# Where the scheduler may reorder a hybrid layer: projection by a timeline model, attention and the down projection in the order they are written

## The chip, the cores and the metric

The kernel runs on one core of a Trainium2 chip. The metric is the device time of one execution in microseconds, as the median of several runs. A core has TensorE (PE, matrix products into the PSUM banks), VectorE (DVE), ScalarE (ACT), GpSimd (POOL) and SyncE (SP, which here issues the DMAs). Each engine works through its own list of instructions in the order of that list, and semaphores hold an instruction until its inputs are there. What the change alters is these lists.

## The reference, cut to what matters

One layer of a decoder trunk, over one sequence of 2048 positions with 1024 channels in float32:

```python
mod = silu(c) @ W_ada + b_ada        # shift, scale and gate, twice
h = RMSNorm(x) * (1 + scale1) + shift1
p = h @ W_in                          # one projection for all head groups
#  A  mLSTM, 4 heads x 64, chunks of 64
#  B  forgetting attention, 8 heads x 64
#  C  spatial gating, 4 groups x 64, chunks of 128
x = x + gate1 * (concat(A, B, C) @ W_out)
h = RMSNorm(x) * (1 + scale2) + shift2
x = x + gate2 * ConvFFN(h)            # up (1024 -> 5632), conv of width 3, SwiGLU, down (2816 -> 1024)

def forgetting_attention(q, k, v, f_pre):     # for each block of 128 queries
    F = cumsum(log_sigmoid(f_pre))
    logits = einsum('bhtd,bhsd->bhts', qb, kb) * scale + F[..., lo:hi, None] - F[..., None, :hi]
    p = softmax(where(mask, logits, -inf))
    out = einsum('bhts,bhsd->bhtd', p, vb)
```

## The kernel before, in words

All products are made in a split form: every operand is cut into a high part hi (fp32r) and a rest lo, and `mm3` (L53 to L56) issues three matmuls, hi·hi, hi·lo and lo·hi. Matmuls named acc belong to the projection, wps to the out-projection, ub to up, db to Down. PSUM tiles are small in number, and each pool of tiles has a fixed count of buffers; an instruction that writes a buffer waits until the last reader of its former content is done.

**Projection** (0 to about 745 us of the trace). Rows of x are normed (ACT squares them, L569, DVE scales them, L571), transposed on PE into tiles trp (L605), and cut into hi and lo. Blocks of weights of w_in come by DMA into wr, ACT makes wh (L652, L676), DVE or POOL makes wl (L653, L677), and PE accumulates. The results are normed (qn L846, vhl L830) and written to DRAM. mLSTM and spatial gating run as lanes between these products. The loop over the steps (L1191 on) is entered, from its second step on, under `tc.manual_schedule` for PE, DVE, ACT and POOL: there these engines' lists follow the program's text. Everything else is put in order by the scheduler of the tile framework, which runs a list schedule against a model of the machine.

**Attention** (about 745 to 1183 us). Heads are taken one after the other; a head is four blocks of 512 query rows, tb = 0 to 3, and block tb attends to (tb + 1) · 512 keys. `scores` makes, for each of four rows of 128 queries, one or two score tiles sp of up to 1024 keys: matmuls (L206, and L210 for the causal mask), a reduction on DVE that adds the forget bias, writes the tile L and tracks the row's minimum nm (L212), and then `exps`: one exp per tile on ACT with its sum rs (L223), the sum's inverse on POOL (L225, L226) and a scaling of the tile on POOL (L228). For tb = 2 and 3 a row has two tiles, so there are eight steps a block, and a row's exps need the reductions of both tiles. `finish` takes the rows of a block and makes, for each 128 keys j, four transposes into a tile tp (L259), a cast phi on ACT (L262), a difference plo on DVE (L263), and, three steps later, two products into op (L245, L246). At the end of a block ACT copies op to yo (L250). PSUM holds two score tiles, three tp and one op. `phase` interleaves the score steps of one block with the finish steps of the block before. Splits of the weights w_out (wo0, L131 and L132) are written between phases of the last heads.

**Out-projection** to 1390 us, **up** to about 2250 us (seven products p of a Strassen-like scheme for each of 22 groups and two halves of the rows, prepared on DVE and ACT: wsph L1467, wspl L1468).

**Down** (about 2241 us to the end). Two halves H of the rows; in each the products p = 1, 2, 7, 6, 5, 4, 3, each of 11 steps k. A step is twelve matmuls of 512 columns into four banks. `prep` makes its operands: sums on DVE (L1577 to L1593, according to p), then for both operands hi on ACT (wsph, L1598) and lo on DVE (wspl, L1599). `prep` is called three steps ahead of `mm`, and the twelve buffers of wsp hold three steps. `post` puts the evictions of a product in the list `later` (copies s1 L1652, sums o, u2 and s1 in L1633 to L1689), and of this list three items are taken after each step. The banks are db0 and db1 in turn; p = 3 goes on accumulating in the tile of p = 5.

## Time and profile before

| | |
|---|---|
| median of 3 runs | 2671.54 us (2666.39 to 2672.4) |
| the profiled execution, time | 2675.71 us |
| the profiled execution, span | 2674.0 us |
| mean granted clock of TensorE | 0.988 |
| POOL busy | 415.6 us, 550 instructions |
| HBM read, written | 274.34 MB, 100.74 MB |

The page of the profile gives for each engine the busy time and its share of the span. A view of stretches gives the same for pieces of the span, with the clock that TensorE was granted there. The view of waits lists, for each place where an engine stood idle, what ended the wait. The timeline lists instructions in order of time: start, duration, engine, line, operation, output and inputs, and in brackets the idle time before it with what ended it. Starts of successive instructions of one engine lie closer than their durations, since they overlap; where a rate matters, the distance of starts is used.

### The profile page before, as it was taken

Reading aid. Unit: us, or ns where it says so; the run is one execution under the profiler, and the core shown is the slowest. Engines: PE = TensorE matmul, PEld = TensorE weight load, DVE = VectorE, ACT = ScalarE, POOL = GpSimd, SP = SyncE. Lnnn points to the kernel's source line nnn. Section 1 sums busy time; section 2 is a strip of 40 time slices with the busy share of each in tenths; the row PEclk is TensorE's granted clock in tenths of the full one; section 3 lists DMA queues with packets and bytes.
Section 4 is the critical chain, followed back from the end, with each engine's and each line's share of the span. In section 5 each row is a group of like instructions: output and inputs, shape, how many; then the busy total and the mean of one; then the engine's idle time right before and its main releaser. Section 6 shows DMA issues by size and latency. Waiting matters only on the chain.

```text
span 2674.0 us, 36818 instructions
## 1 busy us (share of the span) xinstructions
PE 2580.6 (97%) x12761; PEld 2128.9 (80%) x12761; DVE 1992.1 (75%) x3432; ACT 1285.4 (48%) x2442; POOL 415.6 (16%) x550
## 2 busy tenths in 40 slices
PE   5899999999899999999999999999999999999999
PEld 5788787888777877777877888888888888888787
DVE  5555656455448888876749888887988887898797
ACT  3333334333248788874436544444444444444443
POOL 4012210022236566640000000000000000000000
PEclk9899999999999999999999999999999999999999
DMA  7533556424554444536742222228222225748533
GB/s 257 154 117 91 150 152 184 132 70 123 138 171 123 115 133 125 136 98 229 276 142 72 90 84 84 82 84 294 89 85 82 84 79 206 267 148 308 177 101 116
DMA packets 297683, 377.52 MB, mean 141 GB/s; under 512 B 31118, under 2 KB 189676, under 8 KB 295448
## 3 DMA queue, kind: packets, MB, share of 16 engines
q1 hardware_dynamic: 297496, 375.16, 44.4%
q8 instruction: 101, 1.65, 0.3%
q14 instruction: 86, 0.70, 0.1%
HBM read 274.34 MB, written 100.74 MB: 140 GB/s over the span
## 4 chain that ended last, share of the span: by engine, by line
PE 74%; DVE 11%; DMA 5%; ACT 4%; issue 4%; POOL 1%; SPq 0%; DVEq 0%; ACTq 0%; POOLq 0%
PE ub L54 10%; PE ub L56 10%; PE ub L55 10%; PE acc L54 5%; PE acc L56 5%; PE acc L55 5%; PE db L55 4%; PE db L56 4%; PE db L54 4%; PE tp L259 3%; PE sp L206 3%; PE op L245 2%; PE op L246 2%; DVE wspl L1599 2%; DMA x_d<-x 1%
## 5 line engine op out<-in xcount | busy, mean ns | idle before, releaser
L54 PE MATMUL acc<-wh,hh 128*128 128x512 f32 (+2 forms) x768 | 290.8, 379 | 10.9 <-DVE vhl L830 5.3
L55 PE MATMUL acc<-wl,hh 128*128 128x512 f32 (+2 forms) x768 | 277.5, 361 | 4.5 <-POOL wl L677 3.4
L54 PE MATMUL ub<-T,wsph 128*128 128x512 f32 x704 | 274.3, 390 | 5.8 <-ACT wsph L1467 5.8
L56 PE MATMUL acc<-wh,hl 128*128 128x512 f32 (+2 forms) x768 | 278.1, 362 | 0.4 <-DVE hl L611 0.4
L56 PE MATMUL ub<-T,wspl 128*128 128x512 f32 x704 | 273.8, 389 | 0.4 <-DVE wspl L1468 0.4
L55 PE MATMUL ub<-T,wsph 128*128 128x512 f32 x704 | 273.9, 389 | 0.0
L55 PE MATMUL db<-wspl,wsph 128*128 128x512 f32 x616 | 240.4, 390 | 2.2 <-DVE wspl L1599 2.2
L56 PE MATMUL db<-wsph,wspl 128*128 128x512 f32 x616 | 239.6, 389 | 0.0
L54 PE MATMUL db<-wsph 128*128 128x512 f32 x616 | 238.3, 389 | 0.3 <-ACT wsph L1598 0.3
L1467 ACT CAST wsph<-S 128x512 fp32r<-128x512 f32 x176 | 109.7, 623 | 228.6 <-PE ub L55 162.5
L263 DVE TENSOR_TENSOR plo<-tp,phi 128x512 fp32r<-128x512 f32 (+1 forms) x320 | 186.8, 607 | 35.9 <-ACT phi L262 34.0
L54 PE MATMUL ub<-B,wsph 128*128 128x512 f32 x528 | 207.3, 393 | 2.6 <-ACT wsph L1467 2.6
L56 PE MATMUL ub<-B,wspl 128*128 128x512 f32 x528 | 207.0, 392 | 0.8 <-DVE wspl L1468 0.8
L55 PE MATMUL ub<-B,wsph 128*128 128x512 f32 x528 | 207.1, 392 | 0.0
L223 ACT ACTIVATE L<-L,nm 128x1024 f32<-128x1024 f32 (+2 forms) x192 | 172.5, 902 | 32.1 <-DVE nm L212 30.8
L259 PE MATMUL tp<-ident,L 128*128 128x128 f32 x1088 | 178.6, 276 | 5.2 <-DVE vhl L830 1.9
L262 ACT CAST phi<-tp 128x512 fp32r<-128x512 f32 (+1 forms) x320 | 160.1, 521 | 46.0 <-PE tp L259 44.7
L54 PEld LDWEIGHTS acc<-wh,hh 128*128 128x128 f32 x768 | 148.3, 193 | 32.3 <-issue 6.6
L206 PE MATMUL sp<-kk,q 128*128 128x512 f32 (+3 forms) x640 | 168.4, 374 | 2.3 <-DVE nm L212 1.2
L228 POOL TENSOR_SCALAR L<-L,rs 128x1024 f32<-128x1024 f32 (+2 forms) x192 | 167.2, 881 | 11.2
L1598 ACT CAST wsph<-act 128x512 fp32r<-128x512 f32 x132 | 82.2, 623 | 179.0 <-PE db L55 162.6
L55 PEld LDWEIGHTS acc<-wl,hh 128*128 128x128 f32 x768 | 148.2, 193 | 25.1 <-POOL wl L677 3.7
(344 smaller groups left out, 6025.8 us busy)
## 6 DMA issues: line engine op xcount, KB each, us to landing
w<-in_w_up_dram SPq DMA_DIRECT2D x88, 512.0 KB
wd<-in_w_down_dram SPq DMA_DIRECT2D x176, 256.0 KB
wa<-in_w_ada_dram SPq DMA_DIRECT2D x96, 256.0 KB
act_d<-yc SPq DMA_DIRECT2D x44, 512.0 KB
act<-act_d SPq DMA_DIRECT2D x44, 512.0 KB
wr<-in_w_in_dram SPq DMA_DIRECT2D x76, 256.0 KB
q<-q_d SPq DMA_DIRECT2D x128, 128.0 KB
hc_d<-hl SPq DMA_DIRECT2D x28, 512.0 KB
```

The lines of the kernel that those rows point to most:

```text
L54: T.matmul(ps, lh, rh, start=start, stop=False, skip_group_check=resume)
L55: T.matmul(ps, lh, rl, start=False, stop=False, skip_group_check=resume)
L56: T.matmul(ps, ll, rh, start=False, stop=stop, skip_group_check=resume)
L206: T.matmul(sp[:, b : b + bw], q2[n][:, qs], kk[:, s0 + b : s0 + b + bw], start=n == 0, stop=n == 1 and not last)
L223: A.activation(L[c], L[c], AF.Exp, bias=nm[:, n - 1 : n], scale=-1.0, accum_out=rs[:, c : c + 1])
L228: G.tensor_scalar(t, t, rs[:, 0:1], 1.0, op0=ALU.mult, op1=ALU.mult)
L245: T.matmul(op[:, c0:], vv[:, j, :], hi[:, c0:], start=(j == 0), stop=False)
L259: T.transpose(tp[:, i * P : (i + 1) * P], rows[i][j // 8][:, (j % 8) * P : (j % 8 + 1) * P], ident)
L262: A.copy(hi[:, c0:], tp[:, c0:])
L263: V.tensor_tensor(lo[:, c0:], tp[:, c0:], hi[:, c0:].bitcast(F32), op=ALU.subtract)
L1467: A.copy(hi, src)
L1598: A.copy(hi, v)
```

## The change

The scheduler's model is changed for the whole program (`schedule_with_timeline_sim=True`): it now orders against a timeline simulation. The manual schedule of the projection is removed, so that the projection's four engines are ordered by that model too. All PE, DVE, ACT and POOL instructions of attention, and the DVE and ACT instructions of Down, are wrapped in `tc.keep_in_program_order`, called O: each is put behind the one last wrapped on its engine, so that these follow the text among themselves, while other instructions may still go between. In Down the bank counter is also advanced for p = 3, so that the second half begins in the bank that the first half's last product does not hold. No instruction of computation is added or removed; out-projection and up stay free.

```diff
@@ mm3
+    O = tc.keep_in_program_order
@@ scores
-                        T.matmul(
+                        O(T.matmul(
                             sp[:, b : b + bw], q2[n][:, qs], kk[:, s0 + b : s0 + b + bw], start=n == 0, stop=n == 1 and not last
-                        )
+                        ))
...
-                V.tensor_tensor_reduce(
+                O(V.tensor_tensor_reduce(
...
@@ exps
-                    A.activation(L[c], L[c], AF.Exp, bias=nm[:, n - 1 : n], scale=-1.0, accum_out=rs[:, c : c + 1])
+                    O(A.activation(L[c], L[c], AF.Exp, bias=nm[:, n - 1 : n], scale=-1.0, accum_out=rs[:, c : c + 1]))
...
@@ finish
-            A.copy(hi[:, c0:], tp[:, c0:])
-            V.tensor_tensor(lo[:, c0:], tp[:, c0:], hi[:, c0:].bitcast(F32), op=ALU.subtract)
+            O(A.copy(hi[:, c0:], tp[:, c0:]))
+            O(V.tensor_tensor(lo[:, c0:], tp[:, c0:], hi[:, c0:].bitcast(F32), op=ALU.subtract))
...
@@ the projection's loop
-    in_order = tc.manual_schedule(
-        engines={mybir.EngineType.PE, mybir.EngineType.DVE, mybir.EngineType.Activation, mybir.EngineType.Pool}
-    )
     for n, (half, i) in enumerate(steps):
         if n == 1:
-            in_order.__enter__()
...
-    in_order.__exit__(None, None, None)
@@ Down
-                A.copy(hi, v)
-                V.tensor_tensor(lo, v, hi.bitcast(F32), op=ALU.subtract)
+                O(A.copy(hi, v))
+                O(V.tensor_tensor(lo, v, hi.bitcast(F32), op=ALU.subtract))
...
             if k == 0:
+                n_bank[0] += 1
                 if more:
                     self.ps[3] = self.ps[5]
                 else:
-                    n_bank[0] += 1
                     tag = "db%d" % ((n_bank[0] - 1) % 2)
...
-    with tile.TileContext(nc) as tc:
+    with tile.TileContext(nc, schedule_with_timeline_sim=True) as tc:
```

The other instructions of attention and of Down's sums and evictions are wrapped in the same way. Line numbers of the changed kernel are two higher than before in attention and three lower in Down.

## Prediction

> **What bounds the kernel now.** I read the page first, then stretches of the span, then PE's waits, then single stretches of the timeline.

> ```profile
> span 2674.0 us, 36818 instructions
> PE 2580.6 (97%) x12761; PEld 2128.9 (80%) x12761; DVE 1992.1 (75%) x3432; ACT 1285.4 (48%) x2442; POOL 415.6 (16%) x550
> ```

> In the stretches the columns are length, then busy time and instructions of PE, weight loads, DVE, ACT and POOL, granted clock, DMA share, GB/s: the projection's start and end, attention, Down.

> ```profile
> 0.00:50.00 50.00, 23.54 (x110) 21.00 (x110) 32.06 (x52) 18.39 (x43) 31.13 (x42) 0.97 0.87 299
> 50.00:100.00 50.00, 41.98 (x244) 36.60 (x244) 27.10 (x82) 21.84 (x46) 3.50 (x8) 0.84 0.31 97
> 100.00:744.00 644.00, 620.70 (x3366) 519.50 (x3366) 352.57 (x792) 220.01 (x431) 110.25 (x92) 0.98 0.46 136
> 776.00:1183.00 407.00, 397.24 (x2413) 320.79 (x2414) 347.77 (x690) 330.69 (x719) 240.83 (x368) 1.00 0.46 128
> 2241.00:2674.00 433.00, 424.47 (x1864) 348.71 (x1862) 379.21 (x618) 182.32 (x315) 0.00 (x0) 1.00 0.58 197
> 2350.00:2400.00 50.00, 49.20 (x216) 40.03 (x215) 50.00 (x84) 21.38 (x37) 0.00 (x0) 1.00 0.47 153
> ```

> PE sets the end almost everywhere. Its idle time is what another order can win, and it lies early: 26.5 us (50 − 23.54), 8.0 and 23.3 us in the first three rows. Attention has 9.8 us in 407, and Down 8.5 in 433. In Down, DVE is full while PE is nearly full: there the two run neck and neck.

> **Attention, now written order.** The work of one head is four blocks of 512 query rows (tb). For each row of 128 queries DVE reduces one or two score tiles (L212), ACT takes exp of both (L223); each finish step is four transposes, a cast phi on ACT (L262), a difference plo on DVE (L263), and two products three steps later. PE's order is nearly unchanged. DVE's isn't. In the tb=3 block, before:

> ```order
> L212 ISA L_8270,nm_8264<-sp_8265,nf_7473 128x1024
> L212 ISA nm_8264 128x1
> L212 ISA L_8289,nm_8264<-sp_8283,nf_7473,nm_8264 128x768
> L212 ISA nm_8264 128x1
> L263 TENSOR_TENSOR plo_8278<-tp_8272,phi_8277 128x512
> L263 TENSOR_TENSOR plo_8297<-tp_8291,phi_8296 128x512
> ```

> The same two score tiles and two differences on DVE in the changed kernel:

> ```order
> L214 ISA L_8267,nm_8261<-sp_8262,nf_7470 128x1024
> L214 ISA nm_8261 128x1
> L265 TENSOR_TENSOR plo_8275<-tp_8269,phi_8274 128x512
> L214 ISA L_8286,nm_8261<-sp_8280,nf_7470,nm_8261 128x768
> L214 ISA nm_8261 128x1
> L265 TENSOR_TENSOR plo_8294<-tp_8288,phi_8293 128x512
> ```

> A difference now stands between the two reductions of a row. It waits for its phi, which on ACT still stands behind both exps of the row before. So the second reduction, which depends on neither, waits too, and the next row's exps with it: a loop. Its price comes from these rows, DVE's reductions (second parts of successive rows, and one plo), then ACT's exps and a phi of another block:

> ```profile
> 899.49 0.87 DVE L212 CUSTOM_DVE_ANT_0 L<-sp,nf,nm 128x640 f32<-128x640 f32 x1
> ...
> 901.16 0.69 DVE L263 TENSOR_TENSOR plo<-tp,phi 128x512 fp32r<-128x512 f32 x1 [0.79 <-ACT phi L262]
> 901.77 1.21 DVE L212 CUSTOM_DVE_ANT_0 L<-sp,nf 128x1024 f32<-128x1024 f32 x1
> ...
> 903.14 1.02 DVE L212 CUSTOM_DVE_ANT_0 L<-sp,nf,nm 128x768 f32<-128x768 f32 x1
> ...
> 906.64 1.15 DVE L212 CUSTOM_DVE_ANT_0 L<-sp,nf,nm 128x896 f32<-128x896 f32 x1
> ...
> 910.28 1.28 DVE L212 CUSTOM_DVE_ANT_0 L<-sp,nf,nm 128x1024 f32<-128x1024 f32 x1
> ```

> ```profile
> 859.83 0.08 DVE L212 DVE_READ_ACCUMULATOR2_ANT nm<- 128x1 f32 x1
> ```

> ```profile
> 860.01 1.15 ACT L223 ACTIVATE L<-L,nm 128x1024 f32<-128x1024 f32 x1 [0.56 <-DVE nm L212]
> ...
> 861.16 1.14 ACT L223 ACTIVATE L<-L,nm 128x1024 f32<-128x1024 f32 x1
> ...
> 862.29 0.56 ACT L262 CAST phi<-tp 128x512 fp32r<-128x512 f32 x1
> ...
> 882.61 1.04 ACT L223 ACTIVATE L<-L,nm 128x896 f32<-128x896 f32 x1
> ```

> Rows start 3.65, 3.50 and 3.64 us apart before. The loop: reduction's end to exp 0.1 (859.83 + 0.08 to 860.01), two exps 1.15 + 1.13 (start to start; 0.1 to 0.2 less for narrower second parts, as 1.04 against 1.15 shows), phi 0.56 and a hand-over of about 0.05, plo to the next instruction 0.61 (901.16 to 901.77), the second reduction 1.02 to 1.28 and its read 0.08. That is 4.5, 4.75 and 4.9 us: +0.85, +1.25, +1.26, or **+3.3 us a head**. PE can't run ahead, since the score tiles have two buffers and the transposes three. When the block ends, the last row's exps stand ahead of the phi that frees a transpose buffer: 0.25 to see the scores, reduction and read 1.36, 0.1, exps 2.28, phi 0.6, plo 0.69 make 5.3 us. PE has three full finish steps for it and a narrower one, and a full step takes it 0.91 us, as two phis show that waited for PE alone:

> ```profile
> 875.59 0.59 ACT L262 CAST phi<-tp 128x512 fp32r<-128x512 f32 x1 [0.32 <-PE tp L259]
> 876.50 0.59 ACT L262 CAST phi<-tp 128x512 fp32r<-128x512 f32 x1 [0.32 <-PE tp L259]
> ```

> That is 3 × 0.91 + 0.75 = 3.5: **+1.8**. So the tb=3 block alone costs 5.1 a head, 41 us for eight. POOL's scaling in the chain of waits gives the head's period before, 51.67 us:

> ```profile
> 847.33 1.13 POOL L L228
> ...
> 899.00 1.13 POOL L L228
> ```

> The tb=1 block, whose four rows have one tile each, has its turn on ACT; before:

> ```order
> L223 ACTIVATE L_7972,rs_7974<-L_7972,nm_7965 128x768
> L223 ACTIVATE L_7985,rs_7987<-L_7985,nm_7978 128x896
> L262 CAST phi_8009<-tp_8004 128x512
> L223 ACTIVATE L_7998,rs_8000<-L_7998,nm_7991 128x1024
> L262 CAST phi_8019<-tp_8015 128x384
> ```

> And on ACT in the changed kernel:

> ```order
> L225 ACTIVATE L_7969,rs_7971<-L_7969,nm_7962 128x768
> L225 ACTIVATE L_7982,rs_7984<-L_7982,nm_7975 128x896
> L225 ACTIVATE L_7995,rs_7997<-L_7995,nm_7988 128x1024
> L264 CAST phi_8006<-tp_8001 128x512
> L264 CAST phi_8016<-tp_8012 128x384
> ```

> The first phi now waits for the last exp, and that for the last score's reduction: 0.25 + 1.3 + 0.1 + 1.15 + 0.6 + 0.69 = 4.1 us, against 1.6 to 2 us of PE work in the three free transpose buffers (steps of 512, 384 and 256 columns with narrow products, scaled from 0.91): about +2.3. The end of tb=2 is of this kind with narrower tiles; no row shows it, so between 0 and 2. With all four, 9.5 us a head, 76 for eight; some of it replaces waits of before. Between 41 and 76 I take the middle, **+58**. The splits of w_out, written between the blocks, move ahead on ACT in the sixth and seventh heads; each waits for a load, and the pinned exps behind it wait too. No load there was late before, so 0, and up to 5 if one is.

> **Down, DVE and ACT in written order.** Before, in the slack of products p=1 and 2, DVE did sums that later products need:

> ```order
> L1582 TENSOR_TENSOR act_21652<-act_21652,act_21949 128x512
> L1593 TENSOR_TENSOR act_21925<-act_21925,act_21648 128x512
> L1583 TENSOR_TENSOR act_21652<-act_21652 128x512
> L1599 TENSOR_TENSOR wspl_22002<-act_21949,wsph_22001 128x512
> L1582 TENSOR_TENSOR act_21669<-act_21669,act_21973 128x512
> ```

> There the changed kernel's DVE has only the splits of p=1 and 2; where p=7 begins it has:

> ```order
> L1574 TENSOR_TENSOR sw_22334<-act_21690 128x512
> L1576 TENSOR_TENSOR t2w_22336<-wd_22274,wd_22276 128x512
> L1596 TENSOR_TENSOR wspl_22339<-sw_22334,wsph_22338 128x512
> L1596 TENSOR_TENSOR wspl_22343<-t2w_22336,wsph_22342 128x512
> L1630 TENSOR_TENSOR o_22364<-db_22054,s1_22070 128x512
> L1630 TENSOR_TENSOR o_22368<-db_22055,s1_22071 128x512
> L1630 TENSOR_TENSOR o_22372<-db_22056,s1_22072 128x512
> ```

> The sums sit with the product that needs them, and evictions of p=2 in lumps of three between preparations, not one at a time. Steps and DVE instructions have these times (ACT's cast, released by PE, then DVE's):

> ```profile
> 2290.47 0.62 ACT L1598 CAST wsph<-act 128x512 fp32r<-128x512 f32 x1 [1.58 <-PE db L55]
> ...
> 2293.19 0.62 ACT L1598 CAST wsph<-act 128x512 fp32r<-128x512 f32 x1 [1.58 <-PE db L55]
> ```

> ```profile
> 2298.68 0.69 DVE L1579 TENSOR_TENSOR t2w<-wd 128x512 f32<-128x512 f32 x1 [0.21 <-DMA wd<-in_w_down_dram]
> 2299.29 0.69 DVE L1599 TENSOR_TENSOR wspl<-sw,wsph 128x512 fp32r<-128x512 f32 x1
> ```

> PE takes a step each 2.72 us, DVE an instruction each 0.61. Preparation is 2 instructions a step in p=1 and 2, 4 in p=7, 5 in p=6, 3 later. p=7 to 3 need 198 of these and 56 evictions: 254 × 0.61 = 155 us, against 55 × 2.72 = 150 of PE. Before, the order puts 16 of them (9.8 us) early; of the next half's, 8 were done in this stretch, so at least 8 × 0.61 = 5 us a half come back. From above: followed step by step with a lead of 3.5 us (buffers of three steps), p=7 loses 4, p=6 (5 × 0.61 + waits for its own sum = 3.2 a step) 8, p=5 4, p=4 and 3 5: 21 a half. Two halves give 10 to 42; I take **+26**. The swapped bank ends one wait of the second half's p=1 for the first half's last eviction. The view of the tile db has it among the idle times of PE:

> ```profile
> DVE o L1677: 0.2, 1
> ```

> So nothing is won, unless the eviction now comes later; then the other bank covers it.

> [...]

> **Projection, now ordered by the model.** PE's costliest waits here:

> ```profile
> PE trp L605 <- ACT xt L569: 10.9, 4, 7.4
> PE acc L54 <- DVE vhl L830: 5.3, 2, 3.5
> PE acc L54 <- DVE qn L846: 5.1, 1, 5.1
> PE trp L605 <- DVE xt L571: 4.5, 4, 1.3
> ```

> On PE the order moves accumulations in among the first transposes, on ACT the next rows' norms ahead of evictions, and on SP the weights of w_in ahead of later rows of x; of the first 100 us I take 5 to 10 off (the fourth wait of the list and half of the first). Later, 23.3 us idle can at most go, and the model can also put an instruction ahead that waits for a DMA, with all behind it. Bounds −30 and +10; I take **−14**. Out-projection and up are free in both kernels and PE is full in up: 0 ± 5.

> **Sum.** 58 + 26 − 14 = +70 on 2674.0: 2744. The profiled run took 2675.71, 4.2 above the median 2671.54; on the median, **2742**.

> **Rivals.** *The clock falls too.* These rows show a wait and what follows:

> ```profile
> 708.00:712.00 4.00, 1.03 (x7) 0.66 (x5) 1.94 (x4) 1.51 (x4) 1.64 (x1) 1.00 0.70 175
> 712.00:716.00 4.00, 1.91 (x5) 1.55 (x6) 2.16 (x4) 1.07 (x2) 0.00 (x0) 0.60 0.50 135
> ```

> After 3 us idle in 4, the clock is 0.60. If the three block ends of a head do this, 24 × 1.5 us (four at 0.6 lose 1.6) = 36: 2778. Against it: the waits are 2 to 2.5 us, shorter than that one. [...] Chance 0.13.

> *Faster.* The projection's order fills nearly all of PE's waits: 8.0 + 23.3, 5 of the first 50, and the slow clock behind them (0.84 in 50 to 100, 8 us): −44; and attention costs under 20, since the buffers ahead of PE carry it over the waits. It decides at a row time of 4.1 us in tb=3: below, attention adds less than the 44. 2671 − 44 + 20 = 2647. For it: idle is really there. Against: the loop has no buffer in it. 0.09.

> *Small.* Both terms at their floors, 41 + 10 − 14: 2708. 0.17. *The model misjudges DMAs*: +10 instead of −14: 2766. 0.09. *Cancelled*, or the pins move less than the order shows: 2672. 0.04. The forecast: 0.48.

> **How the numbers follow.** Measurement tells about 0.2%, 5 us. All but the faster and the cancelled case are slower: 0.48 + 0.13 + 0.17 + 0.09 = 0.87; same 0.04, faster 0.09. From the small case less 5 for the free stages' spread and 10 for a better projection, 2692; up to 2795, the clock's case and half of the way from the taken to the upper values of attention and Down (9 + 8).

> **Right or wrong.** In the changed profile: second reductions 4.5 to 4.9 us apart with an idle DVE waiting for phi; a head of 57 to 61 us against 51.7; PE waits in Down for wspl of 10 or more a half; PE busier before 744. Row times near 3.7 would undo the main term, and a PE still full at p=6 the second.

## The result and the profile after

The changed kernel takes 2804.26 us (median of 4 runs, 2801.99 to 2807.38) against 2670.07 for the kernel before: a ratio of 1.0505, 95% interval 1.0486 to 1.0523. The prediction was 2742, with a range up to 2795: right in its sign, and off in size, since the loss is 134 us where 70 were forecast. In the profiled execution the head of the page reads

```profile
span 2800.3 us, 36772 instructions
PE 2614.0 (93%) x12745; PEld 2138.5 (76%) x12761; DVE 2004.6 (72%) x3432; ACT 1293.3 (46%) x2441; POOL 414.2 (15%) x550
```

PE is busy for 33 us more than before (2580.6) with the same matmuls, and idle for 93 us more. The second is waits; the first is for the greater part a slower clock, as is worked out below. The two have to be told apart in each stage. Stages are cut at the last matmul into acc, the first into wps, the first into ub and the first into db:

| stage, us | before | after | difference | of it PE idle | of it PE busy |
|---|---|---|---|---|---|
| projection, to the last acc | 774.1 | 733.8 | −40.3 | −21.8 | −18.5 |
| attention, to the first wps | 408.9 | 516.2 | +107.3 | +75.2 | +32.1 |
| out-projection, to the first ub | 207.2 | 214.3 | +7.1 | +6.6 | +0.5 |
| up, to the first db | 851.3 | 852.6 | +1.3 | +0.1 | +1.2 |
| Down, to the end | 432.5 | 483.4 | +50.9 | +32.8 | +18.1 |

The stretches of the changed kernel that answer to those shown of before (50 to 100 us, attention, Down):

```profile
50.00:100.00 50.00, 46.88 (x288) 42.58 (x289) 39.70 (x93) 24.87 (x47) 1.65 (x3) 0.95 0.67 211
733.80:1250.00 516.20, 429.69 (x2416) 333.41 (x2414) 355.71 (x694) 339.82 (x722) 240.23 (x368) 0.94 0.37 102
2316.90:2800.30 483.40, 442.04 (x1861) 353.64 (x1859) 392.30 (x616) 184.45 (x315) 0.00 (x0) 0.97 0.50 173
```

The clock in attention is 0.94 where it was 1.00, and the busy time of its 2416 matmuls is 429.7 where it was 397.6. In the view of PE's waits over the whole run, the four lines at the top are new in size (before: 0.4, 0.3, 1.2 and 4.1 us), and so is a wait for a DMA (before: 0.2). The columns are us in total, times, longest:

```profile
PE tp L261 <- DVE plo L265: 49.3, 45, 3.1
PE db L54 <- ACT wsph L1595: 34.3, 28, 2.9
PE sp L208 <- DVE nm L214: 12.3, 21, 1.1
PE op L247 <- ACT yo L252: 12.1, 16, 1.3
...
PE sp L208 <- DMA q<-q_d: 8.8, 2, 8.0
```

The loop of the prediction is there. In a tb=3 block the second reductions on DVE, and the differences that stand ahead of them, read

```profile
829.08 0.88 DVE L214 CUSTOM_DVE_ANT_0 L<-sp,nf,nm 128x640 f32<-128x640 f32 x1
...
832.63 0.69 DVE L265 TENSOR_TENSOR plo<-tp,phi 128x512 fp32r<-128x512 f32 x1 [0.91 <-ACT phi L264]
833.24 1.01 DVE L214 CUSTOM_DVE_ANT_0 L<-sp,nf,nm 128x768 f32<-128x768 f32 x1
...
837.62 1.14 DVE L214 CUSTOM_DVE_ANT_0 L<-sp,nf,nm 128x896 f32<-128x896 f32 x1
...
842.25 1.27 DVE L214 CUSTOM_DVE_ANT_0 L<-sp,nf,nm 128x1024 f32<-128x1024 f32 x1
...
906.98 1.27 DVE L214 CUSTOM_DVE_ANT_0 L<-sp,nf,nm 128x1024 f32<-128x1024 f32 x1
```

Rows start 4.16, 4.38 and 4.63 us apart (before 3.65, 3.50, 3.64; 4.5, 4.75 and 4.9 were forecast), and DVE stands idle for the phi ahead of each second reduction. The last line is the same place one head later: a head takes 64.7 us, where 57 to 61 were forecast and 51.7 is the time before.

At the end of the block PE waits for the transpose buffer, as forecast. Three such waits in PE's timeline, two at the end of a tb=1 block and, in the middle, one at the end of a tb=3 block (at the first the profile names a load of q; one head later the same wait is put down to plo):

```profile
808.05 0.33 PE L261 MATMUL tp<-ident,L 128*128 128x128 f32 x1 [2.09 <-DMA q<-q_d]
...
844.80 0.40 PE L248 MATMUL op<-plo,vv 128*128 128x512 f32 x1
847.24 0.69 PE L261 MATMUL tp<-ident,L 128*128 128x128 f32 x2 [2.04 <-DVE plo L265]
847.58 0.78 PE L247 MATMUL op<-phi,vv 128*128 128x512 f32 x1
...
1141.60 0.33 PE L261 MATMUL tp<-ident,L 128*128 128x128 f32 x1 [2.09 <-DVE plo L265]
```

What happens then is seen in stretches of 3.41 us around these waits (the clock stands after POOL's column):

```profile
805.77:809.18 3.41, 1.23 (x7) 0.81 (x6) 1.76 (x4) 2.91 (x7) 3.21 (x5) 1.00 0.41 126
809.18:812.60 3.42, 2.55 (x9) 1.98 (x8) 1.57 (x4) 0.00 (x0) 0.15 (x1) 0.50 0.36 77
812.60:816.01 3.41, 3.41 (x13) 2.83 (x13) 1.48 (x5) 2.21 (x5) 1.41 (x3) 0.50 0.00 0
...
843.32:846.73 3.41, 1.20 (x6) 0.58 (x5) 1.04 (x4) 3.11 (x6) 1.49 (x3) 1.00 0.94 232
846.73:850.14 3.41, 2.90 (x11) 2.41 (x12) 2.23 (x5) 1.25 (x4) 2.38 (x3) 0.50 1.02 226
...
1136.86:1140.28 3.42, 2.65 (x20) 2.16 (x18) 2.16 (x4) 2.99 (x7) 3.13 (x6) 1.00 0.25 76
1140.28:1143.69 3.41, 2.00 (x10) 1.55 (x10) 1.76 (x4) 1.95 (x6) 2.51 (x3) 1.00 0.83 227
1143.69:1147.10 3.41, 2.33 (x16) 1.91 (x15) 2.45 (x5) 1.53 (x4) 0.00 (x0) 1.00 0.86 240
```

With the first two of these waits, of 2.09 and 2.04 us, the clock goes to half; with the third, of 2.09 us, it does not. In this trace the clock changes only at instants that are multiples of 3.41 us apart (809.18, 816.01, 846.73 and 850.14 in these rows). Call the time between two such instants a slice. The first wait lies in one slice, in which PE is busy for 1.23 of 3.41 us, and the clock is at half from 809.2 to 816.0. Of the second wait 1.5 us lie in a slice that holds shorter ones too, with PE busy for 1.20, and the clock is at half from 846.7 to 850.1. The third wait is as long as the first, but two slices share it (2.65 and 2.00 busy), and the clock stays up. A product of 512 columns takes 0.78 us at half clock (L247 at 847.58), where the same line takes 0.48 at full clock (844.49).

In attention 64.9 us run at half clock, in 13 stretches (before: 3.4 us). PE is busy in 51.6 of them, and half of that, 26 us, is an estimate of what the clock costs, 24 more than before. The other 8 of the 32 us of busy time are not slower work. Records of successive matmuls overlap (twelve of 0.39 us take 2.72 us in a step of Down), and where PE has to wait, the tail of one record, about 0.16 us, lies bare. Attention has 103 gaps of over 0.05 us where it had 46; 57 tails are an estimated 9 us. In Down PE is busy for 22.4 us at half clock, where before has none, so by the same estimate 11 of the 18 us are the clock.

In Down, p=6 on DVE goes

```profile
2418.05 0.68 DVE L1579 TENSOR_TENSOR act<-act 128x512 f32<-128x512 f32 x1
2418.77 0.69 DVE L1580 TENSOR_TENSOR act<-act 128x512 f32<-128x512 f32 x1
2419.38 0.69 DVE L1581 TENSOR_TENSOR t2w<-t2w,wd 128x512 f32<-128x512 f32 x1
2420.23 0.69 DVE L1596 TENSOR_TENSOR wspl<-act,wsph 128x512 fp32r<-128x512 f32 x1 [0.16 <-ACT wsph L1595]
2420.84 0.68 DVE L1596 TENSOR_TENSOR wspl<-t2w,wsph 128x512 fp32r<-128x512 f32 x1
2421.44 0.68 DVE L1579 TENSOR_TENSOR act<-act 128x512 f32<-128x512 f32 x1
```

3.39 us a step (3.2 were forecast), with PE needing 2.72. PE waits in Down for the cast wsph (34.3 us, in the view above), not for wspl, as the forecast's sign had it: the cast on ACT stands behind the sum of its own step, and that sum behind DVE's earlier work.

### The profile page after: what moved, and what is told of

Read it like the earlier page. It is cut to its first block, busy times and chain, and to the rows that moved or that the text cites. A ratio compares the mean times of both kernels' runs of the same rounds, so it can differ in the third digit from the quotient of the medians.

```text
span 2800.3 us, 36772 instructions
## 1 busy us (share of the span) xinstructions
PE 2614.0 (93%) x12745; PEld 2138.5 (76%) x12761; DVE 2004.6 (72%) x3432; ACT 1293.3 (46%) x2441; POOL 414.2 (15%) x550
## 3 DMA queue, kind: packets, MB, share of 16 engines
q8 instruction: 100, 1.64, 0.2%
## 4 chain that ended last, share of the span: by engine, by line
PE 69%; DVE 11%; DMA 7%; ACT 6%; issue 6%; SPq 0%; POOL 0%; ACTq 0%; DVEq 0%; POOLq 0%
PE ub L55 10%; PE ub L54 10%; PE ub L56 10%; PE acc L54 6%; PE acc L55 6%; PE acc L56 6%; PE sp L208 3%; PE db L54 2%; DVE wspl L1596 2%; PE db L55 2%; PE db L56 2%; PE tp L261 2%; ACT L L225 2%; DMA ld<-y_d 2%; DVE L L214 2%
## 5 line engine op out<-in xcount | busy, mean ns | idle before, releaser
L54 PE MATMUL acc<-wh,hh 128*128 128x512 f32 (+2 forms) x768 | 283.7, 371 | 9.2 <-DVE qn L848 6.1
L55 PE MATMUL acc<-wl,hh 128*128 128x512 f32 (+2 forms) x768 | 275.5, 361 | 0.0
L54 PE MATMUL ub<-T,wsph 128*128 128x512 f32 x704 | 273.1, 390 | 2.3 <-ACT T L1290 1.8
L55 PE MATMUL ub<-T,wsph 128*128 128x512 f32 x704 | 274.2, 390 | 0.6 <-DVE T L1291 0.6
L265 DVE TENSOR_TENSOR plo<-tp,phi 128x512 fp32r<-128x512 f32 (+1 forms) x320 | 188.7, 608 | 116.7 <-ACT phi L264 114.3
L55 PE MATMUL db<-wspl,wsph 128*128 128x512 f32 x616 | 244.4, 397 | 0.0
L225 ACT ACTIVATE L<-L,nm 128x1024 f32<-128x1024 f32 (+2 forms) x192 | 172.0, 897 | 95.9 <-DVE nm L214 91.2
L54 PE MATMUL ub<-B,wsph 128*128 128x512 f32 x528 | 207.5, 393 | 8.0 <-ACT s L1491 4.1
L55 PE MATMUL ub<-B,wsph 128*128 128x512 f32 x528 | 207.1, 392 | 0.0
L54 PE MATMUL db<-wsph 128*128 128x512 f32 x616 | 172.7, 401 | 34.3 <-ACT wsph L1595 34.3
L261 PEld LDWEIGHTS tp<-ident,L 128*128 128x128 f32 x1088 | 130.3, 144 | 90.5 <-DVE plo L265 69.8
L264 ACT CAST phi<-tp 128x512 fp32r<-128x512 f32 (+1 forms) x320 | 158.4, 518 | 87.2 <-PE tp L261 85.9
L54 PEld LDWEIGHTS db<-wsph 128*128 128x128 f32 x616 | 115.2, 191 | 70.9 <-ACT wsph L1595 48.3
L54 PEld LDWEIGHTS acc<-wh,hh 128*128 128x128 f32 x768 | 146.5, 191 | 29.5 <-issue 5.2
L230 POOL TENSOR_SCALAR L<-L,rs 128x1024 f32<-128x1024 f32 (+2 forms) x192 | 166.3, 875 | 12.6
```

The costliest lines, as they stand in the source:

```text
L54: T.matmul(ps, lh, rh, start=start, stop=False, skip_group_check=resume)
L55: T.matmul(ps, lh, rl, start=False, stop=False, skip_group_check=resume)
L225: O(A.activation(L[c], L[c], AF.Exp, bias=nm[:, n - 1 : n], scale=-1.0, accum_out=rs[:, c : c + 1]))
L230: O(G.tensor_scalar(t, t, rs[:, 0:1], 1.0, op0=ALU.mult, op1=ALU.mult))
L261: O(T.transpose(tp[:, i * P : (i + 1) * P], rows[i][j // 8][:, (j % 8) * P : (j % 8 + 1) * P], ident))
L264: O(A.copy(hi[:, c0:], tp[:, c0:]))
```

## The experiments

Theory A: the written order makes the loss in each stage by itself, by waits that stand ahead of independent work on DVE and ACT, and PE's clock, falling after such waits, adds to it. Rival B: part of the loss comes from the timeline model (loads, ends of stages), or from the plain count of DVE's instructions. All stage times are cut as in the table. Where no interval is given, it is one execution. How far one execution carries can be seen from stages that were the same program: attention of the changed kernel took 516.2, 517.9 and 520.1 us in three traces, Down 483.4, 484.0 and 484.2.

**Attention pinned alone** in the kernel before:

```diff
+    O = tc.keep_in_program_order
 # O(...) around the PE, DVE, ACT and POOL instructions of scores, exps and finish; all else as before
```

> The kernel before, with only attention's instructions pinned to the written order (default machine model, projection's manual schedule kept, Down free). Theory A, the written order itself makes the loss and the half-speed clock behind its block ends doubles it: the stretch from the projection's last accumulation to the first matmul of the out-projection grows from 409 us by 90 to 107 us, time 2760 to 2780, clock in attention 0.90 to 0.97. Theory B, the written order costs what the prediction's rows gave and the rest of the loss comes from the other model (late q loads, other places of the w_out splits): that stretch grows by 55 to 65 us, time 2725 to 2740.

```profile
772.20:1283.90 511.70, 431.34 (x2416) 337.35 (x2414) 355.23 (x694) 339.78 (x722) 240.76 (x368) 0.93 0.37 102
```

2779.56 us. Attention takes 511.7 us (+102.8), projection 772.2 and Down 432.6 as before. Theory A: nearly all of attention's loss, clock included, is the written order; 4.5 us are left for the model, hardly more than the spread just given. The 7.7 us wait for q is here too, so it is not the model's.

**Down pinned alone**, with the bank swap:

```diff
 # O(...) around DVE and ACT of class Down, n_bank[0] += 1 for p == 3; all else as before
```

> The kernel before, with only VectorE and ScalarE of Down pinned and the bank swapped. Theory A, Down's written order alone makes Down's loss: Down lasts 475 to 485 us against 432, time 2715 to 2727, everything else as before. Theory B, half of Down's loss comes from what the timeline model does with up's end and the loads: Down grows by 26 us or less, time at most 2700.

```profile
2239.20:2717.20 478.00, 438.25 (x1861) 348.81 (x1859) 392.80 (x617) 184.58 (x315) 0.00 (x0) 0.98 0.53 178
```

2718.98 us; Down 478.0 (+45.5 of the 50.9). Theory A. The swapped bank cannot be seen: its 0.2 us are far under what a run can tell.

**No pins, timeline model for all** (this and the edits up to the sums one step ahead are made in the changed kernel):

```diff
-    O = tc.keep_in_program_order
+    O = lambda ins: ins
```

> The changed kernel with no pins at all: the timeline model orders attention and Down too, bank swap kept. Theory A, the pins make the whole loss: the projection ends about 40 us earlier than before as in the changed kernel, attention lasts 400 to 425 us and Down 425 to 440 us, time 2615 to 2655. Theory B, the model's own order is as bad as the written one there, which would be a reason for pins: attention over 480 us or Down over 470, time over 2700.

2713.46 us, and each theory is right in one place. Attention takes 413.3 us: there the model's own order is good, and the pins are nearly the whole loss. (The stretch holds 57 matmuls fewer than that of the changed kernel, 2359 for 2416; they stand behind the first matmul of the out-projection, whose stretch has 55 more.) Down takes 481.5 us: there the model's order is as bad as the written one, with this line at the head of PE's waits:

```profile
PE db L55 <- DVE wspl L1596: 27.5, 25, 3.0
```

Out-projection takes 223.8 us (207.2 before).

**Whole rows in the written order:**

```diff
@@ phase
             next(sc)
+            if n_sc == 8 and n % 2 == 0:
+                continue
             while done < (n + 1 - lead) * (n_fin - 5) // (n_sc - lead):
```

> The changed kernel with one edit in the written order: in blocks tb=2 and tb=3 finish steps come only after both score tiles of a row, not between them. Theory A, the loop is reduction, exps, phi, plo, reduction: second reductions of tb=3 fall from 4.2 to 4.6 us apart to 3.5 to 3.8, 15 to 30 us in all, time 2772 to 2790; the waits at block ends and the half clock stay. Theory B, rows wait for something else (score tiles, POOL): second reductions stay over 4.1 us apart, time within 8 us of 2804.

```profile
826.91 0.88 DVE L214 CUSTOM_DVE_ANT_0 L<-sp,nf,nm 128x640 f32<-128x640 f32 x1
...
829.69 1.02 DVE L214 CUSTOM_DVE_ANT_0 L<-sp,nf,nm 128x768 f32<-128x768 f32 x1
...
833.20 1.15 DVE L214 CUSTOM_DVE_ANT_0 L<-sp,nf,nm 128x896 f32<-128x896 f32 x1
...
836.85 1.29 DVE L214 CUSTOM_DVE_ANT_0 L<-sp,nf,nm 128x1024 f32<-128x1024 f32 x1
```

2769.99 us; the last rows are 3.51 and 3.65 us apart, the loop is gone, and attention falls by 35 us to 481.1, a little more than expected: PE's busy time falls by 14 us with it (429.7 to 415.3). What is left is 72 us over before; the next run shows how much of it the ends of blocks are.

**Finish steps carried into the next block,** on top of whole rows:

```diff
@@ phase
+        n_fin += carried[0]
...
-        for _ in fin:
-            pass
+        if now and then:
+            carried[:] = n_fin - done, fin      # run first in the next phase
+        else:
+            for _ in fin:
+                pass
```

> As the run with whole rows, and the last five finish steps of a block are no longer run off behind the block's last score but carried into the next block, between its scores. Theory A, the waits of about 2 us at block ends are left over from that run-off, and they halve TensorE's clock for some microseconds after each: attention falls from 481 us to 415 to 445, its clock from 0.95 to 0.99 or 1.00, TensorE's busy time there from 415 to about 398 us. Theory B, the clock falls for other reasons (many short waits, the share of transposes): clock stays below 0.97 and busy time above 408 us even where idle time falls.

```profile
734.50:1156.20 421.70, 389.43 (x2406) 320.73 (x2405) 351.50 (x691) 339.88 (x720) 243.64 (x370) 0.98 0.45 124
```

2712.1 us. Attention takes 421.7 us; a head in the middle takes 50.9 (before 51.7), measured like the 64.7 above. Waits at block ends and the slow clock go down together, with no other edit: PE waits 11.2 us for plo where it waited 32.0, the mean clock of the stage is 0.98 where it was 0.95, and PE's busy time falls from 415.3 to 389.4. If the clock is either full or half, as in the traces of the two kernels, these means stand for about 48 and 17 us at half; with PE busy in four fifths of the difference, as in the changed kernel's slow time (51.6 of 64.9), the clock is an estimated 12 of these 26 us. The rest was not split further. The mean clock of 0.98 lies just under theory A's 0.99. Of the 12.8 us left over before, one wait for q, 8.9 us at the beginning, is most: in the changed kernel, where it is 8.0 us, the loads of q (from 738.01) stand on SP behind a load of vv (737.52), which waits for the store of the projection's last values (1.1 us in the view of SP's waits).

**Down, one eviction a step:**

```diff
-        for _ in range(1 if s[0] == "up" else 3):
+        for _ in range(1):
```

> The changed kernel, in Down one item of the list of evictions is taken after each step, not three. Theory A, the lumps of evictions between preparations are what VectorE loses by in written order: Down falls from 483 us to 450 to 468, the clock there from 0.97 to 0.98 or more. Theory B, the plain number of instructions for p=7 to p=3 (254 of 0.61 us against 150 us of PE) is the limit, wherever they stand: Down stays at 475 or more.

2800.49 us; Down 477.5, only 5.9 less. Theory B here: the lumps of evictions, with which the prediction described DVE's new order, are not what costs most.

**And the sums of the first four steps early:**

```diff
+            if p == 2 and 4 <= k < 8:
+                self.early[k - 4] = self.sums(7, k - 4)
+                self.sums(6, k - 4)
+                self.sums(3, k - 4)
...
# sums(p, k) holds the sums of prep for p=7, 6 and 3, which leave prep for k < 4; one eviction a step as above
```

> As the run with one eviction at a time, and the sums of the first four steps of p=7, 6 and 3 are written in p=2, where the scheduler had put them in the kernel before. Theory A: with 16 instructions a half out of the crowded stretch and no lumps, Down is within 12 us of the kernel before's 432. Theory B, the hi casts behind the sums of the other steps (DVE, ACT, DVE in each step) hold PE anyway: Down stays above 455.

2782.4 us; Down 457.8, another 19.7 less: 16 instructions a half, moved out of the crowded stretch, are 9.8 us a half or 19.6 in all. This matches. But 457.8 is above theory A's 444 and also above theory B's 455: casts behind the sums of the other steps still hold PE, which waits 16.6 us for wsph.

**Attention left to the model, Down mended so far:**

```diff
 # early sums and one eviction a step as above, O only in class Down
```

> Pins in Down alone, with its order mended as in the run with early sums; attention left to the timeline model. If stages add as they have so far: projection to 740, attention 413, out-projection 224, up 853, Down 432 to 445: 2662 to 2677, the same as the kernel before or a few us better, since what the model wins in the projection it gives back in the out-projection.

2689.36 us, 12 above the upper figure, since Down is 458.6 here too and not 432 to 445. The other stages come as put in (738.7, 412.0, 224.9, 853.4).

**Sums one step ahead of their casts,** with both mended orders:

```diff
@@ the loop over steps
+        n = steps[i + AHEAD + 1] if i + AHEAD + 1 < len(steps) else ("",)
+        if n[0] == "dn" and n[2:] in downs[n[1]].B:
+            downs[n[1]].pre(n[2], n[3])      # the sums of prep, without its casts and differences
         prep(i + AHEAD)
...
```

> The timeline model and the pins, with both written orders mended: attention as in the run with carried finish steps; Down with early sums, one eviction a step, and the sums of a step written one step ahead of its casts and differences, so that no difference waits on VectorE behind a sum and a cast of its own step. Theory A, in-order waits of VectorE for the cast behind its own sum are what keeps Down 25 us above 432: Down falls to 432 to 445, and the sum of stages is 734 + 422 + 216 + 854 + 438 = 2664, a ratio of 0.994 to 1.000. Theory B, VectorE's total is the limit: Down stays at 452 or more, time over 2676.

```profile
2228.60:2671.60 443.00, 426.62 (x1861) 347.70 (x1859) 386.15 (x616) 182.73 (x315) 0.00 (x0) 1.00 0.56 189
```

2670.46 us, a ratio of 0.9999 (0.9989 to 1.0009). Down falls by 14.8 us to 443.0, its clock is 1.00: the wait for the cast behind its own sum was the greater part of what was left, and 10.5 us over before remain. So with a written order that follows the engines' queues the loss is gone in sum. But the projection's 40 us are gone as well: attention +12.6, out-projection +11.4, Down +10.5 and up +3.0 over before take 37.5 of them.

**The manual schedule removed, and nothing else:**

```diff
-    in_order = tc.manual_schedule(engines={PE, DVE, Activation, Pool})
-            in_order.__enter__()
-    in_order.__exit__(None, None, None)
```

> The kernel before with only the projection's manual schedule removed: default model, everything else as before. It tells what the projection's 40 us come from. Theory A, from freeing the four engines, whatever the model: the projection ends at 730 to 745 us instead of 774, attention, out-projection, up and Down stay as before (409, 207, 851, 432), time 2630 to 2645, faster than both kernels. Theory B, from the timeline model's times: the default model, left free, puts instructions ahead that wait, the projection ends at 774 or later, time 2670 or more.

2647.48 us, a ratio of 0.9906 (0.9885 to 0.9927): faster than both kernels, by a little under 1%. The projection ends at 747.7 us, and the time is 2.5 us over theory A's range; attention takes 411.9, out-projection 205.7, up 852.6 and Down 433.5. So some 26 of the projection's 40 us come from freeing its engines (the same pinned projection ended at 770.5, 772.2 and 774.1 us in three traces), 14 come with the timeline model, and only the first keep the other stages whole. The timeline model with the manual schedule kept was not run. The rows of before and this run from 50 to 100 us show where it begins (before, in the prediction: PE busy 41.98, clock 0.84):

```profile
50.00:100.00 50.00, 45.69 (x268) 41.27 (x268) 36.53 (x91) 24.76 (x47) 1.84 (x4) 0.88 0.61 191
```

**The same, with attention pinned in its mended order:**

```diff
 # default model, no manual schedule; whole rows and carried steps, O around attention
```

> Default model, projection freed, and attention alone pinned in the mended written order (whole rows, finish steps carried on); Down and everything else free as before. Theory A, stages add and the mended order is as good as its 50.9 us a head against 51.7 in the kernel before: attention falls from 412 to 402 to 408 us, time 2638 to 2645 against 2647 for the freed projection alone. Theory B, the pins cost at attention's ends (first loads of q, the splits of w_out), which took 12 us in the run with carried steps: attention 415 to 425, time 2650 to 2662, and the free order is the better one.

2652.46 us, 0.9926 (0.9913 to 0.9940). Attention is 412.4 us, as with the free order, between the ranges of the two theories; the time lies in theory B's. What the shorter heads win, a wait of 7.9 us for q at the beginning takes. The intervals of this and of the run before overlap; the simpler one stands.

## Why the prediction was right or wrong

**The bound and the places: right.** Attention and Down were named as the stages that lose, by DVE's and ACT's order, the projection as the one that wins; pinned alone, each loses as much as in the changed kernel, less 5 us.

**Attention's idle time: +58 taken, 75 measured,** at the forecast's upper end of 76. The loop was right and over-priced (+2.4 us a head by the three rows, not 3.3). Each distance was charged with the second reduction of the row behind it, where the loop runs through that of the row ahead: in the last distance 1.07 us (837.62 to its read at 838.69) and not 1.28; and the two exps took 2.17 us (838.87 to the phi at 841.04) and not 2.28. The ends of blocks were under-priced. Taken one by one they were right (1.8 and 2.3 us forecast, 2.04 and 2.09 measured), but the middle of the bounds left them about 4 us a head, and without the wait for q and the loop nearly 6 of idle time are measured. I treated part of them as replacing waits of before, but before had hardly any: 11 us idle in the whole of attention. Some 8 us are the wait for q at the start, which was not foreseen: the scores that need q come first in the written order, and the transposes that had covered the same wait come later.

**The clock: the step that failed.** "*The clock falls too*" stood among the rivals with 36 us and a chance of 0.13, as if it were another way that it could go, and the sum had nothing for it. It comes on top of the waits: PE's busy time grows by 32 us in attention and 18 in Down, of which an estimated 24 and 11 are the clock itself. With these 50 us the sum would have been 2792. The reason given against it, that waits of 2 to 2.5 us are shorter than the one of 3 us whose aftermath was quoted, was a guess: the trace shows falls behind waits of 2.04 and 2.09 us. That the rival's 36 us come near the 32 of attention is luck: it took 24 falls of 1.5 us each, and the trace has 13 stretches at half clock, the longest of 13.7 us in and behind the wait for q, which was not foreseen; and it had nothing for Down. In the trace a slice of 3.41 us in which PE was still busy for 1.23 us (from 805.77), or even for 1.63, 48% (from 1102.7), was followed by half speed.

**Down: +26 taken, 33 of idle time measured,** and 18 of busy time. The lumps of evictions, which the working put between the preparations, were a small part: one at a time gave 6 us. The parts that held are the sums that were hoisted before (20 us of 51, where the lower bound had 10) and the casts behind their own sums (15); some 10 stay unexplained.

**Projection: −14 taken, −40 measured,** outside the bound of −30. The bound was PE's idle time that seemed removable after the first 50 us, and of idle time 22 us went, inside it. It left out the clock, which in 50 to 100 us was 0.84 before and 0.95 with the waits filled: 18 us of busy time went too. Only the faster rival had counted that. It is the same omission as above, in the other direction.

**What hid what.** On the spans, attention and Down lost 158 us where the sum had 84, out-projection and up 8 where it had none, and the projection won 40 where it had 14. The first two errors, 83 us, and the last, 26, have opposite signs; that the sum was off by 56 and not by 83 is luck.

**The bank swap and up: right,** nothing and 1 us. The out-projection lost 7 us under the timeline model, outside the ±5 given for it and up (17 without pins, but with 55 matmuls more in its stretch).

**What stays open:** why the timeline model's own order of Down is as bad as the written one was not looked into, nor what the last 10 us of Down in the mended order are. Whether a pin stands behind the last pinned instruction only, or behind whatever was written last on its engine, no run here tells.

## What to carry to other kernels

Price a new wait of PE twice: its length, and the busy time that comes with it, which here added 32 us to 75 and 18 to 33, an estimated 24 and 11 of them from half speed behind the wait; and price a wait that goes in the same way. Where an engine takes its list in order, as DVE does here (0.91 us idle for a phi at 832.63, the reduction behind it only at 833.24), an instruction that waits is charged for everything behind it that was ready: look for the loop that runs through two engines' queues (reduction, exp, cast, difference, reduction), and write sums a step ahead of what waits for their casts. When a change has several parts, run the part that frees something alone: here it was worth 0.9%, hidden under 5% of loss.

## What the runs showed of the hardware that was not expected

Gaps of one length had different prices: in the changed kernel one of 2.09 us that ended at 808.05 was followed by 6.8 us at half clock, one of 2.04 us that ended at 847.24 came with 3.4 us at half (846.7 to 850.1), and one of 2.09 us that ended at 1141.60 had no fall behind it. In before, a gap of 1.92 us that ended at 776.40 was followed by a mean clock of 0.71 from 776 to 780.
